# FFN channel units as three 256-column products in one PSUM bank, and another place for the input in SBUF

## The chip, the core and the metric

The kernel runs on one core of a Trainium2 chip. A core has five engines that run their own instruction streams and meet only at semaphores: TensorE (PE) multiplies matrices, ScalarE (ACT) applies functions, VectorE (DVE) does elementwise arithmetic, GpSimd (POOL) and SyncE (SP) do the rest; here SP starts all the DMA transfers. A matmul on PE has a stationary operand (the weights of the array, loaded by an instruction of its own, LDWEIGHTS, shown as PEld in the profile) and a moving operand that streams through the array, one column at a time. Both are read from SBUF, the on-chip memory of 128 partitions; the sum goes to PSUM, which has eight banks of 2 KB per partition (512 fp32 numbers each).

The metric is the device time of one execution in microseconds (us); lower is better.

## The reference

The reference is a decoder trunk of two layers over 256 tokens of width 1024. Each layer is a half-step SwiGLU feed-forward (FFN), a token mixer, and a second half-step FFN; a final norm ends it.

```
def swiglu(x, w_in, w_out):
    gate, up = jnp.split(x @ w_in, 2, axis=-1)
    return (jax.nn.silu(gate) * up) @ w_out
...
    for l in range(DEPTH):
        h = h + 0.5 * swiglu(rms_norm(h, ffn1_norm[l]), ffn1_w_in[l], ffn1_w_out[l])
        u = rms_norm(h, mix_norm[l])
        ...
        h = h + merged @ w_out[l]
        h = h + 0.5 * swiglu(rms_norm(h, ffn2_norm[l]), ffn2_w_in[l], ffn2_w_out[l])
    return rms_norm(h, final_norm)
```

The hidden width of the FFN is 2816. The mixer projects its normed input to many channels, runs a Mamba-2 branch and a gated DeltaNet branch on them, and merges the two. All is float32.

## The kernel before

**Precision.** PE takes float32 in a fast format (float32r) that keeps fewer bits. So each operand is split into a high and a low part, and a product `w * u` is computed as three: `wh * uh`, `wh * ul`, `wl * uh`. `mm3` (L287 to L289) does it with the activations as the stationary operand, `mm3w` (L292 to L294) with the weights as the stationary operand.

**The input.** Each of the four FFNs and two mixers begins with `norm_in`. It norms the 256 tokens, transposes them and writes their high and low parts to one tile, `uT`, of shape 128 partitions x 8 (blocks of 128 input channels, `KT`) x 2 (high, low) x 256 tokens. In a partition, the high and the low part of one block lie next to each other, so they can also be read as one run of 512 columns. `uT` is in the pool `cpool`, which is allocated ahead of the pools of the weights (`wpool`) and of the activations (`slots`, `s2`).

**The weights.** SP loads them in tiles of 128 x 1024 (`wraw`); ACT copies each one to `whi` and DVE subtracts to get `wlo`, both float32r, in five buffers each. `take()` hands out the next pair and has later ones loaded and split (up to five ahead). Weights come in the order of the products, so PE's program order is the order of everything.

**Products of the input.** There are two kinds. A token chunk (`tok_chunk`) has `uT` stationary, 128 tokens at a time, and 512 columns of weights moving: outputs `t0`, `t1` in the mixer, `f0`, `f1` at the start of an FFN. A channel chunk has 128 x 128 weights stationary and `uT` moving, so the output lies with channels in partitions. In the mixer that is `chan_chunk`: for each of two groups of 128 channels and each of the eight blocks, `mm3w`, which is three matmuls of 256 columns, into one half of a single PSUM bank (outputs `kk`, `qq`, `vv`, `zd`, `bc`, `xs`). In the FFN it is `chan_pair`: for each group and block one matmul of 512 columns (L342, `wh` with high and low part side by side) and one of 256 columns (L346, `wl` with the high part, onto the first 256 columns of the same bank), so each group of 128 channels fills a whole bank, and `both` adds the two halves afterwards.

**A channel unit of the FFN.** For each of the 20 units of an FFN, the first group of 128 channels is the gate and the second the up part. ACT copies the second half of the gate's bank to `sg`, DVE adds the first half, ACT applies SiLU; ACT copies the second half of the up bank to `g2`, DVE adds the first half, and DVE multiplies the two. Two units make one `g2`, which `split` turns into a high part `gh` and a low part `gl`, and `block_sums` into sums for a blocked product (`bsa`, `bsb`, `bsc`, `bsd`). The string `FFN` sets the order: `f` the token chunk, `c` a channel unit, `A` and `B` blocked products with w_out, `d` direct ones. An `A` uses channel units that ended at least two units before. The PSUM pool `accp` has four banks, taken in turn; the pool `trp` has the other four.

**The mixer.** The string `ORDER` is its order, written out by hand; the channel units there are followed by a convolution on ACT and DVE (tile `ca`).

The lines that the change touches:

Of the kernel before, what the change touches and what calls it, by code (L numbers as in the profile page):

```python
# [8 lines left out]
F32R = mybir.dt.float32r  # L9
# [7 lines left out]
P = 128  # L17
# [12 lines left out]
NRAW = 5  # L30
NSPL = 5
START = 2

# [18 lines left out]
def trunk_kernel(ctx, tc, x, wst, wsm, norms, lpar, rpar, cst, out):  # L52
# [12 lines left out]
    def act(o, i, func=AF.Copy, **kw):  # L65
        return A.activation(out=o, in_=i, func=func, **kw)  # L66

    def tt(o, a, b, op):
        return V.tensor_tensor(out=o, in0=a, in1=b, op=op)  # L69
# [18 lines left out]
    def accb(name):  # L88
        return accp.tile([P, 512], F32, tag="acc", name=name)
# [91 lines left out]
    def take():  # L181
        j = state["taken"]
        state["taken"] = j + 1
        ahead("loaded", min(plan[min(j + NSPL, n_forms) - 1][2] + NRAW - 1, n_raw), load)
        ahead("prepped", min(j + 1 if state["hold"] else j + NSPL, n_forms), prep)
        return halves.pop(j)
# [40 lines left out]
    Y = [cpool.tile([P, 512], F32, name=f"Y{i}") for i in range(2)]  # L227
    for y in Y:
        G.memset(y[:], 0.0)
    uT = cpool.tile([P, KT, 2, S], F32R, name="uT")  # L230
    uTh, uTl = uT[:, :, 0], uT[:, :, 1]

    def rstd_of(t):

# [25 lines left out]

    def norm_in(nw, add=None):

        for t in range(2):
            with tc.high_priority(offset=PRI), ExitStack() as behind:
                if add:
                    add(t)
                    if t == 0:
                        behind.enter_context(tc.issue_after(state["sums"][5].ins))
                ins, done = rms_chain(t, nw)
            if t == 0:  # L270
                state["hold"] = False
                n = state["taken"]
                if not add:
                    ahead("prepped", n + 1, prep)
                    with tc.issue_after(done[0].ins), tc.issue_after(done[1].ins):
                        ahead("prepped", n + START, prep)
                with tc.issue_after(ins.ins):
                    ahead("prepped", n + 2, prep)
                if add:
                    state["behind"][n + 2] = [d.ins for d in done]  # L280
            elif add:

                state["behind"][n + 4] = (state["square"].ins, ins.ins)
                state["input"] = done
# [28 lines left out]
    def chan_chunk(ps):  # L313

        ws = [take(), take()]
        for a in range(2):
            for q in range(2):
                wh, wl = ws[q]
                for k in range(4):
                    kt = 4 * q + k  # L320
                    c0 = k * 256 + a * P
                    mm3w(
                        ps[:, a * 256 : (a + 1) * 256],
                        wh[:, c0 : c0 + P],
                        wl[:, c0 : c0 + P],
                        uTh[:, kt, :],
                        uTl[:, kt, :],
                        kt == 0,
                        kt == KT - 1,
                    )  # L330

    def chan_pair(ps):


        ws = [take(), take()]
        for a in range(2):
            for q in range(2):
                wh, wl = ws[q]
                for k in range(4):
                    kt = 4 * q + k  # L340
                    c0 = k * 256 + a * P
                    PE.matmul(  # L342
                        ps[a][:], wh[:, c0 : c0 + P], uT[:, kt].rearrange("p o t -> p (o t)"),
                        start=kt == 0, stop=False,
                    )
                    PE.matmul(ps[a][:, 0:S], wl[:, c0 : c0 + P], uTh[:, kt, :], start=False, stop=kt == KT - 1)  # L346
            yield a

    def both(o, ps):
        act(o, ps[:, S : 2 * S])  # L350
        return tt(o, ps[:, 0:S], o, ALU.add)

    def out_chunks(ps, stat, ks, last, group=1, split=False, first=None):

# [86 lines left out]
    def ffn(nxt):  # L441
        gh = [slots.tile([P, 8, S], F32R, tag=t_, name="gh") for t_ in ("sA", "sB", "sC")]
        gl = [slots.tile([P, 8, S], F32R, tag=t_, name="gl") for t_ in ("sD", "sE", "sF")]

        bsa = slots.tile([P, 2, 2, 3, P], F32R, tag="sG", name="bsa")
        bsb = slots.tile([P, 16, P], F32R, tag="sH", name="bsb")
        bsc = slots.tile([P, 4, 2, P], F32R, tag="sI", name="bsc")
        bsd = s2.tile([P, 2, 2, P], F32R, tag="s2", name="bsd")
        bsb3 = bsb[:, 0:12].rearrange("p (i o j) t -> p i o j t", i=2, o=2)
        bsb1 = bsb[:, 12:16].rearrange("p (i o) t -> p i o t", i=2)  # L450

        def sums(p, j):

            q, i = (p - 1) // 2, (p - 1) % 2
            if j < 3:
                b = (bsa[:], bsb3)[q % 2]
                return b[:, i, 0, j, :], b[:, i, 1, j, :]
            b = (bsc[:, 0:2], bsc[:, 2:4], bsb1, bsd[:])[q]
            return b[:, i, 0, :], b[:, i, 1, :]

        def block_sums(p, g2):

            sf = tmp2("sf")
            a11, a21, a12, a22 = (g2[:, j * P : (j + 1) * P] for j in range(4))
# [12 lines left out]
            tt(l1, s4, f(h1), ALU.subtract)  # L477

        def split(k0, bv):
            oh = gh[k0 // 8][:, k0 % 8 : k0 % 8 + 2, :]  # L480
            ol = gl[k0 // 8][:, k0 % 8 : k0 % 8 + 2, :]
            act(oh, bv)
            tt(ol, bv, f(oh), ALU.subtract)

        def stat(k, t):
            return (gh[k // 8][:, k % 8, t * P : (t + 1) * P], gl[k // 8][:, k % 8, t * P : (t + 1) * P])

        ps = [accb("f0"), accb("f1")]
        tok_chunk(ps, range(KT))
        gt = []  # L490
        for t in range(2):
            sg = tmp2("sg")
            act(sg[:, 0:256], ps[t][:, 0:256], AF.Silu)
            tt(sg[:, 256:512], sg[:, 0:256], ps[t][:, 256:512], ALU.mult)
            gt.append(sg[:, 256:512])
        todo, pb, n = FFN[1:], {}, 0
        for c in range(FC - 1):
            g2 = tmp2("g2")
            for a in range(2):
                pc = [accb("fc"), accb("fc")]  # L500
                sg = s2.tile([P, S], F32, tag="ca", name="sg", bufs=2)
                gv = g2[:, a * S : (a + 1) * S]
                for i in chan_pair(pc):
                    if i == 0:
                        both(sg[:], pc[0])
                        act(sg[:], sg[:], AF.Silu)
                both(gv, pc[1])
                tt(gv, sg[:], gv, ALU.mult)
                todo = todo[1:]
                if c == 0 and a == 0:  # L510
                    bank = trb("gT")
                    for k in range(2):
                        for t in range(2):
                            PE.transpose(bank[:, k * S + t * P : k * S + (t + 1) * P], gt[t][:, k * P : (k + 1) * P], ident)
                    split(0, bank[:].rearrange("p (k t) -> p k t", k=2))
            split(2 * c + 2, g2[:].rearrange("p (k t) -> p k t", k=2))
            if c + 1 <= PAIRS[-1][-1]:
                block_sums(c + 1, g2)
            if todo[0] == "A":
                if not pb:  # L520
                    pb.update({i: trb(f"p{i}") for i in (1, 6, 5, 7)})
                four = [
                    (pb[1], lambda p: stat(2 * p, 0), PAIRS[n]),
                    (pb[5], lambda p: sums(p, 0), PAIRS[n]),
                    (pb[7], lambda p: sums(p, 2), PAIRS[n]),
                    (pb[6], lambda p: sums(p, 1), PAIRS[n]),
                ]
                block_products(four, n == 0, n == len(PAIRS) - 1)
                todo = todo[1:]
                n += 1  # L530
        po = [[accb("o"), accb("o")] for _ in range(2)]

        return close_blocks(po, stat, sums, pb, nxt)
# [841 lines left out]
```

## Time and profile before

| | |
|---|---|
| median of 3 runs | 1570.2 us (1566.86 to 1570.4) |
| span of the profiled execution, first to last instruction | 1565.8 us |
| what lies around the span, against the median | 4.4 us |
| mean granted TensorE clock | 0.999 |
| PE busy | 1545.0 us, 10152 matmuls |
| DVE busy | 1302.4 us |
| ACT busy | 999.8 us |
| DMA | 292.99 MB, 55.2% of the DMA engines' time |

The profiled execution's time is its span, 1565.8 us, and the little that lies ahead of the first and behind the last instruction; the three runs are 1.1 to 4.6 us above the span.

How to read it: "busy" of PE is counted from the start of each matmul to its modelled end, and matmuls overlap, so a matmul of 512 columns shown with 390 ns does not take 390 ns of PE's time. What a stream of matmuls takes is the distance from one start to the next, and that is read from the start times in the timeline. In a row of the groups, "L342 PE MATMUL fc<-uT,whi 128\*128 128x512 f32 x1280" is line 342, output `fc`, operands `uT` and `whi`, a stationary operand of 128 x 128, 512 moving columns, 1280 instructions; then busy time, mean ns of one, and the idle time of the engine ahead of them. The four FFNs begin with their token chunks at about 10, 604, 787 and 1379 us; the mixers begin at about 193 and 969 us.

### The profile page before, as it was taken

To read this page: it belongs to the slowest core of one execution; us is meant where nothing else is said; L and a number is where in the kernel's file an instruction comes from. 1 tells how busy PE (TensorE), PEld (TensorE's weight loads), DVE (VectorE), ACT (ScalarE), POOL (GpSimd) and SP (SyncE) were. 2 spreads that over 40 slices of the span, in tenths; PEclk is the share of its full clock that TensorE was granted. 3 is DMA by queue.
4 is the path that set the end of the run, shared out by engine and by line. 5 is a ranking of instruction groups with operands and counts; after the bars stand their busy time and mean duration, and the time that the engine had idled before them with its cause. 6 is when DMAs were issued, how large, how long until landed. Compare 5 with 4: busy or idle time off the path is not lost.

```text
span 1565.8 us, 26672 instructions
## 1 busy us (share of the span) xinstructions
PE 1545.0 (99%) x10152; PEld 1342.0 (86%) x10152; DVE 1302.4 (83%) x2048; ACT 999.8 (64%) x1694; POOL 53.2 (3%) x60
## 2 busy tenths in 40 slices
PE   8999999999999999999999999999999999999998
PEld 6888779999888888888788887899998888888886
DVE  6889969957899766899878998699579996679897
ACT  6666668766675655666566676686656666466664
POOL 0000010000000000000000001010000000000000
PEclk9999999999999999999999999999999999999999
DMA  8565565553455555465765566555336546555553
GB/s 298 197 214 188 195 212 173 178 158 118 174 207 173 177 205 196 159 210 177 262 204 187 168 198 223 189 189 189 116 123 213 177 166 212 201 175 166 198 189 134
DMA packets 94215, 292.99 MB, mean 187 GB/s; under 512 B 22325, under 2 KB 23301, under 8 KB 93062
## 3 DMA queue, kind: packets, MB, share of 16 engines
q1 hardware_dynamic: 94086, 291.29, 55.2%
q8 instruction: 79, 1.29, 0.3%
q14 instruction: 50, 0.41, 0.1%
HBM read 289.33 MB, written 1.92 MB: 186 GB/s over the span
## 4 chain that ended last, share of the span: by engine, by line
PE 76%; DVE 13%; DMA 5%; issue 3%; ACT 2%; POOL 1%; SPq 0%; POOLq 0%; DVEq 0%; ACTq 0%
PE fc L342 15%; PE fc L346 8%; DVE wlo L69 7%; PE t L287 3%; PE t L288 3%; PE t L289 3%; DMA wraw<-in_wst_dram 3%; PE b L289 3%; PE b L288 3%; PE b L287 2%; PE xs L292 2%; PE xs L293 2%; PE xs L294 2%; PE o L288 1%; PE o L289 1%
## 5 line engine op out<-in xcount | busy, mean ns | idle before, releaser
L69 DVE TENSOR_TENSOR wlo<-wraw,whi 128x1024 fp32r<-128x1024 f32 x488 | 591.0, 1221 | 139.8 <-ACT whi L66 136.1
L66 ACT ACTIVATE whi<-wraw 128x1024 fp32r<-128x1024 f32 x488 | 511.6, 1057 | 176.4 <-PE b L289 29.8
L342 PE MATMUL fc<-uT,whi 128*128 128x512 f32 x1280 | 445.5, 391 | 0.0
L346 PE MATMUL fc<-uT,wlo 128*128 128x256 f32 x1280 | 360.9, 282 | 0.0
L342 PEld LDWEIGHTS fc<-uT,whi 128*128 128x128 f32 x1280 | 240.3, 188 | 50.7
L346 PEld LDWEIGHTS fc<-uT,wlo 128*128 128x128 f32 x1280 | 241.8, 189 | 0.8
L287 PE MATMUL t<-whi,uT 128*128 128x512 f32 x256 | 102.9, 403 | 0.0
L288 PE MATMUL t<-wlo,uT 128*128 128x512 f32 x256 | 101.5, 396 | 0.2 <-DVE wlo L69 0.2
L289 PE MATMUL t<-whi,uT 128*128 128x512 f32 x256 | 101.5, 397 | 0.0
L66 ACT ACTIVATE whi<-wfirst 128x1024 fp32r<-128x1024 f32 x64 | 67.8, 1059 | 29.7 <-DVE wfirst L69 20.4
L66 ACT ACTIVATE sg<-fc 128x256 f32<-128x256 f32 x80 | 30.6, 382 | 82.3 <-PE fc L346 82.3
L69 DVE TENSOR_TENSOR wlo<-wfirst,whi 128x1024 fp32r<-128x1024 f32 x64 | 78.1, 1220 | 2.0 <-ACT whi L66 1.9
L287 PE MATMUL b<-whi,bh 128*128 128x512 f32 x192 | 76.1, 398 | 0.0
L288 PE MATMUL b<-wlo,bh 128*128 128x512 f32 x192 | 74.9, 390 | 0.0
L289 PE MATMUL b<-whi,bl 128*128 128x512 f32 x192 | 74.3, 394 | 0.3 <-DVE bl L69 0.3
L292 PE MATMUL xs<-uT,whi 128*128 128x256 f32 x256 | 73.1, 286 | 0.0
L294 PE MATMUL xs<-uT,wlo 128*128 128x256 f32 x256 | 71.6, 280 | 0.0
L293 PE MATMUL xs<-uT,whi 128*128 128x256 f32 x256 | 71.4, 279 | 0.0
L288 PE MATMUL o<-wlo,gh 128*128 128x512 f32 x160 | 64.6, 404 | 2.6 <-DVE wlo L69 2.5
L69 DVE TENSOR_TENSOR wfirst<-wraw,wfirst 128x1024 f32<-128x1024 f32 x48 | 58.6, 1220 | 8.9 <-DMA wraw<-in_wst_dram 8.9
L289 PE MATMUL o<-whi,gl 128*128 128x512 f32 x160 | 62.5, 391 | 0.0
L287 PE MATMUL o<-whi,gh 128*128 128x512 f32 x160 | 62.1, 392 | 0.0
(317 smaller groups left out, 3424.5 us busy)
## 6 DMA issues: line engine op xcount, KB each, us to landing
wraw<-in_wst_dram SPq DMA_DIRECT2D x504, 512.0 KB, 4.5
wfirst<-in_wst_dram SPq DMA_DIRECT2D x16, 512.0 KB, 5.8
dc<-rdram SPq DMA_DIRECT2D x8, 1024.0 KB, 8.4
nw<-in_norms_dram SPq DMA_DIRECT2D x6, 512.0 KB, 6.2
gb<-rdram SPq DMA_DIRECT2D x8, 256.0 KB, 5.3
h<-in_x_dram SPq DMA_DIRECT2D x4, 256.0 KB, 5.7
out_dram<-fo SPq DMA_DIRECT2D x4, 256.0 KB, 2.1
dq<-X SPq DMA_DIRECT2D x2, 256.0 KB, 5.0
```

The costliest lines, as they stand in the source:

```text
L66: return A.activation(out=o, in_=i, func=func, **kw)
L69: return V.tensor_tensor(out=o, in0=a, in1=b, op=op)
L287: PE.matmul(ps, lh, rh, start=start, stop=False)
L288: PE.matmul(ps, lh, rl, start=False, stop=False)
L289: return PE.matmul(ps, ll, rh, start=False, stop=stop)
L292: PE.matmul(ps, wh, mh, start=start, stop=False)
L293: PE.matmul(ps, wh, ml, start=False, stop=False)
L294: PE.matmul(ps, wl, mh, start=False, stop=stop)
L342: PE.matmul(ps[a][:], wh[:, c0 : c0 + P], uT[:, kt].rearrange("p o t -> p (o t)"), start=kt == 0, stop=False,)
L346: PE.matmul(ps[a][:, 0:S], wl[:, c0 : c0 + P], uTh[:, kt, :], start=False, stop=kt == KT - 1)
```

## The change

1. The FFN's channel units use `chan_chunk`, as the mixer's do: three matmuls of 256 columns in place of one of 512 and one of 256, with gate and up in the two halves of one bank. `chan_pair` and `both` go. SiLU reads the gate from PSUM, and the multiplication reads the up part from PSUM.
2. The tile of the input has 64 more elements per partition (256 bytes), and the input lies 40 elements (160 bytes) behind its start, in each of the six norms. With this the weight tiles lie 64 bytes behind the input modulo 256. All tiles allocated after it move by 256 bytes, so their places modulo 256, and the distances between them, stay.

```
+PLACES = 6 * [40]
...
-    uT = cpool.tile([P, KT, 2, S], F32R, name="uT")
-    uTh, uTl = uT[:, :, 0], uT[:, :, 1]
+    uW = cpool.tile([P, KT * 2 * S + 64], F32R, name="uW")
+    uT = uTh = uTl = None
+    places = list(PLACES)
+
+    def place_input():
+        nonlocal uT, uTh, uTl
+        o = places.pop(0)
+        uT = uW[:, o : o + KT * 2 * S].rearrange("p (k o t) -> p k o t", k=KT, o=2)
+        uTh, uTl = uT[:, :, 0], uT[:, :, 1]
...
     def norm_in(nw, add=None):
 
+        place_input()
...
-    def chan_pair(ps):
...
-                    PE.matmul(
-                        ps[a][:], wh[:, c0 : c0 + P], uT[:, kt].rearrange("p o t -> p (o t)"),
-                        start=kt == 0, stop=False,
-                    )
-                    PE.matmul(ps[a][:, 0:S], wl[:, c0 : c0 + P], uTh[:, kt, :], start=False, stop=kt == KT - 1)
...
-    def both(o, ps):
-        act(o, ps[:, S : 2 * S])
-        return tt(o, ps[:, 0:S], o, ALU.add)
...
-                pc = [accb("fc"), accb("fc")]
+                ps = accb("fc")
+                chan_chunk(ps)
                 sg = s2.tile([P, S], F32, tag="ca", name="sg", bufs=2)
-                gv = g2[:, a * S : (a + 1) * S]
-                for i in chan_pair(pc):
-                    if i == 0:
-                        both(sg[:], pc[0])
-                        act(sg[:], sg[:], AF.Silu)
-                both(gv, pc[1])
-                tt(gv, sg[:], gv, ALU.mult)
+                act(sg[:], ps[:, 0:S], AF.Silu)
+                tt(g2[:, a * S : (a + 1) * S], sg[:], ps[:, S : 2 * S], ALU.mult)
```

`chan_chunk`, which stays as it is:

```
        ws = [take(), take()]
        for a in range(2):
            for q in range(2):
                wh, wl = ws[q]
                for k in range(4):
                    kt = 4 * q + k
                    c0 = k * 256 + a * P
                    mm3w(
                        ps[:, a * 256 : (a + 1) * 256],
                        wh[:, c0 : c0 + P], wl[:, c0 : c0 + P],
                        uTh[:, kt, :], uTl[:, kt, :],
                        kt == 0, kt == KT - 1,
                    )
```

More of the change, by code (lines that the diff above doesn't have):

```diff
@@ L330, in chan_chunk @@
                     )
-    def chan_pair(ps):
[L335 to L342, printed above, removed]
-                        ps[a][:], wh[:, c0 : c0 + P], uT[:, kt].rearrange("p o t -> p (o t)"),
-                        start=kt == 0, stop=False,
-                    )
-                    PE.matmul(ps[a][:, 0:S], wl[:, c0 : c0 + P], uTh[:, kt, :], start=False, stop=kt == KT - 1)
-            yield a
-    def both(o, ps):
-        act(o, ps[:, S : 2 * S])
-        return tt(o, ps[:, 0:S], o, ALU.add)
     def out_chunks(ps, stat, ks, last, group=1, split=False, first=None):
```

## The prediction

> **What bounds the kernel now.** I read the page's busy times and its chain first.
>
> ```profile
> span 1565.8 us, 26672 instructions
> PE 1545.0 (99%) x10152; PEld 1342.0 (86%) x10152; DVE 1302.4 (83%) x2048; ACT 999.8 (64%) x1694; POOL 53.2 (3%) x60
> PEclk9999999999999999999999999999999999999999
> PE 76%; DVE 13%; DMA 5%; issue 3%; ACT 2%; POOL 1%; SPq 0%; POOLq 0%; DVEq 0%; ACTq 0%
> ```
>
> PE is busy almost throughout, the clock is full everywhere, and three quarters of the chain that ends last are PE's. So the question is how fast PE's stream of matmuls goes, and whether the next engine, DVE at 83%, lets it go faster. The stretches, by the windows (span of time; then busy us and count of PE, PEld, DVE, ACT, POOL; clock; DMA):
>
> ```profile
> 33.00:69.00 36.00, 36.00 (x209) 31.91 (x209) 30.39 (x56) 22.39 (x41) 0.00 (x0) 1.00 0.61 206
> 234.00:262.00 28.00, 28.00 (x242) 28.00 (x242) 26.10 (x55) 21.99 (x37) 0.00 (x0) 1.00 0.57 194
> 440.00:505.00 65.00, 64.94 (x502) 57.14 (x500) 62.46 (x81) 42.35 (x56) 3.07 (x2) 1.00 0.55 187
> ```
>
> The first is FFN channel units alone: PE never pauses, DVE has 30.39 of 36 us. The second is mixer channel units: DVE 26.10 of 28. The third is the densest part of the mixer for DVE, 62.46 of 65: there DVE sets the pace as much as PE does.
>
> The groups say how many matmuls read the input, which the change moves:
>
> ```profile
> L342 PE MATMUL fc<-uT,whi 128*128 128x512 f32 x1280 | 445.5, 391 | 0.0
> L346 PE MATMUL fc<-uT,wlo 128*128 128x256 f32 x1280 | 360.9, 282 | 0.0
> L292 PE MATMUL xs<-uT,whi 128*128 128x256 f32 x256 | 73.1, 286 | 0.0
> L292 PE MATMUL bc<-uT,whi 128*128 128x256 f32 x128 | 36.7, 287 | 0.0
> L292 PE MATMUL zd<-uT,whi 128*128 128x256 f32 x128 | 36.3, 284 | 0.0
> L292 PE MATMUL vv<-uT,whi 128*128 128x256 f32 x128 | 36.0, 281 | 0.0
> L292 PE MATMUL qq<-uT,whi 128*128 128x256 f32 x128 | 36.0, 281 | 0.0
> L292 PE MATMUL kk<-uT,whi 128*128 128x256 f32 x128 | 35.9, 281 | 0.0
> L287 PE MATMUL t<-whi,uT 128*128 128x512 f32 x256 | 102.9, 403 | 0.0
> L287 PE MATMUL f<-whi,uT 128*128 128x512 f32 x64 | 26.4, 415 | 0.5 <-ACT uT L66 0.5
> ```
>
> FFN channel units: 1280 pairs of 512 and 256 columns. Mixer channel units: the six L292 rows are 896 matmuls, and L293 and L294 have as many, so 2688 of 256 columns. Token chunks: 256 + 64 on each of three lines, 960 of 512 columns with `uT` stationary.
>
> **What each kind costs now.** From start times in the timeline (start us, modelled us), first row of a stretch and first row behind it:
>
> ```profile
> 130.01 0.40 PE L342 MATMUL fc<-uT,whi 128*128 128x512 f32 x1
> 141.12 0.39 PE L287 MATMUL p<-whi,gh 128*128 128x512 f32 x1
> 319.76 0.28 PE L292 MATMUL zd<-uT,whi 128*128 128x256 f32 x1
> 325.36 0.28 PE L292 MATMUL bc<-uT,whi 128*128 128x256 f32 x1
> 439.06 0.40 PE L287 MATMUL t<-whi,uT 128*128 128x512 f32 x1
> 450.27 0.38 PE L1045 MATMUL xsb<-cs,xsT 128*128 128x128 f32 x2
> 98.27 0.39 PE L287 MATMUL p<-whi,bsb 128*128 128x512 f32 x1
> 102.35 0.40 PE L342 MATMUL fc<-uT,whi 128*128 128x512 f32 x1
> ```
>
> - FFN: two units, 32 pairs, in 141.12 - 130.01 = 11.11 us: 347.2 ns for a pair (768 columns).
> - Mixer: one unit, 48 matmuls of 256, in 5.60 us: 116.7 ns each, 350.0 for the same 768 columns.
> - Token chunks: two units, 48 matmuls of 512, in 11.21 us: 233.5 ns each.
> - Blocked products: 18 matmuls of 512, in 4.08 us: 226.7 ns each.
>
> The last two are the same matmul in shape, type and clock, and differ by 6.8 ns. What differs is where the operands lie. After the change the weights are 64 bytes behind the input modulo 256, and the input moves by 160, so before they are 64 + 160 = 224 bytes behind it, or 32 ahead: 32 off a multiple of 64. `bsb` and the weights are a whole multiple of 256 bytes apart, as the tiles between them have 4096, 6144 and 8192 bytes. So in this trace a half-step distance costs time and a whole one costs none, which also fits the other rows: take 226.7 / 512 = 0.4428 ns a column as the price of columns alone, and 768 columns cost 340.0. The FFN pair is 7.2 over that with two matmuls, the mixer's three are 10.0 over: 3.6 and 3.3 ns for a matmul with `uT` moving, 6.8 with `uT` stationary.
>
> **The change, part by part.**
>
> *Three products for a pair, alone:* the same columns, one more matmul and one more weight load (1280 in all). At the mixer's price, 350.0 - 347.2 = 2.8 ns more a pair: 1280 x 2.8 = +3.6 us, on the path, as PE has no pause there.
>
> *The new place:* 64 bytes is a whole step of 64, so if the step is what counts, each kind falls to the price of columns: 340.0 for three, 113.3 for 256, 226.7 for 512. No row shows this distance: the aligned rows are all at 0 modulo 256. Bounds from the nearest rows: 0 for a matmul as in the `p` rows, and 6.8 for each as in the `t` rows, the dearest that a distance costs here. A price below 0 has no row behind it, though nothing excludes it. I take 0, since at 64, as at 0, both operands cross 64-byte steps together. Then:
>
> - FFN: 1280 x (347.2 - 340.0) = 9.2 us, the 3.6 of the first part already in it.
> - Mixer channel units: 2688 x (116.7 - 113.3) = 9.1 us.
> - Token chunks: 960 x (233.5 - 226.7) = 6.5 us.
>
> Together 24.8 us of PE time. Two deductions. In 440:505 DVE has no room, and its counterpart in the second mixer neither; 64 matmuls on each of the three channel lines and about 43 of `t` lie in it: 192 x 3.4 + 43 x 6.8 = 0.95 us, twice, 1.9. And an aligned stream takes a few matmuls to settle:
>
> ```profile
> 96.89 0.39 PE L287 MATMUL p<-whi,gh 128*128 128x512 f32 x1
> 97.12 0.40 PE L288 MATMUL p<-wlo,gh 128*128 128x512 f32 x1
> 97.36 0.39 PE L289 MATMUL p<-whi,gl 128*128 128x512 f32 x1
> 97.59 0.39 PE L287 MATMUL p<-whi,gh 128*128 128x512 f32 x1
> ```
>
> The first three take 0.70 us, 0.02 over three at the settled price (0.68). The mixers have 2688 / 48 = 56 channel and 768 / 24 = 32 token units; if each begins unsettled, that is 88 x 0.02 = 1.8 us. Net: 24.8 - 1.9 - 1.8 = 21.1.
>
> *The evacuation:* ACT and DVE lose work in the 80 units.
>
> ```profile
> L66 ACT ACTIVATE sg<-sg 128x256 f32<-128x256 f32 x80 | 33.0, 413 | 22.4 <-DVE sg L69 21.9
> L66 ACT ACTIVATE sg<-fc 128x256 f32<-128x256 f32 x80 | 30.6, 382 | 82.3 <-PE fc L346 82.3
> L66 ACT ACTIVATE g<-fc 128x256 f32<-128x256 f32 x80 | 29.4, 367 | 0.1
> L69 DVE TENSOR_TENSOR g<-sg,g 128x256 f32<-128x256 f32 x80 | 33.7, 421 | 0.5
> L69 DVE TENSOR_TENSOR sg<-fc,sg 128x256 f32<-128x256 f32 x80 | 33.6, 420 | 4.1 <-ACT sg L66 4.0
> L69 DVE TENSOR_TENSOR g<-fc,g 128x256 f32<-128x256 f32 x80 | 33.5, 419 | 0.0
> L66 ACT ACTIVATE sg<-f 128x256 f32<-128x256 f32 x8 | 3.1, 384 | 3.6 <-PE f L289 3.6
> ```
>
> ACT has one SiLU from PSUM (384, as `sg<-f`) in place of 382 + 413 + 367: 62 us less over the kernel. DVE has one multiplication of about 420 in place of three: 67 us less. I cost both at 0: PE has no pause in 33:69, so there is nothing for it to gain; the worth is that DVE, at 30.39 of 36, doesn't become the bound when PE runs 2% faster.
>
> *One bank for gate and up:* ACT may now have to wait for all 48 matmuls, where it had its first bank after half of them; the 82.3 us of idle time ahead of `sg<-fc` would grow, and the splits of weights queued behind it on ACT would come later. Cost 0: splits run up to five tiles ahead, two and a half units, and an `A` reads units that ended two units before. Without that cover it is 384 + 420 = 0.8 us a unit. Four banks now hold four units, where they held two, so a bank comes free earlier than before.
>
> *The rest:* `place_input` issues nothing. No DMA changes; PE's faster pace asks for the same bytes in 1.4% less time, with the DMA engines at 0.61. Tiles behind the input move by 256 bytes, so their distances stay.
>
> The sum against the profiled execution: span 1565.8 - 21.1 = 1544.7, and with the 4.4 us by which the median of the three runs is over that span 1549.1. I predict 1549.
>
> **The rivals.**
>
> *The place does nothing.* The difference between `t` and `p` rows would then come from the token chunks' own pattern of operands, and only the third product counts: +3.6 us, 1574. Against it stands that mixer and FFN channel units, with the operands' parts exchanged, are over the price of columns too. Chance 0.14. The Trainium skill speaks for it, in "SBUF — State Buffer", "A bandwidth-pool intuition that's wrong (but worth ruling out)": PE's weight loads have a read port of their own, independent of the moving operand's, so by that page the distance between the two shouldn't matter. In "TensorE: Matmul & The Clock Gate", "Back-to-back issue gap", a warm matmul alone takes its columns at 2.4 GHz and 2.5 ns; by that page the estimate is 2.5 ns for each of the 1280 added, +3.2 us, and nothing for the place. The trace doesn't agree with either: the same shape takes 226.7 or 233.5, both over that page's 215.8.
>
> *64 is a bad distance (slower).* Both operands would meet at the same step of a store with more than one step to its cycle, on every matmul. For it speaks that an aligned stream that hasn't settled pays too (0.24 us for one of 512, from 97.12 to 97.36). At the dearest row's price, 6.8, a 256-column matmul takes 120.1: FFN 1280 x (360.3 - 347.2) = +16.8, mixer 2688 x 3.4 = +9.1, token chunks 0; 1596. It decides as soon as a matmul of 256 costs over 347.2 / 3 = 115.7 in the FFN. Against it: `p` settles within three matmuls. Chance 0.14.
>
> *Half of it.* Streams of 256 settle only partly, at 115: FFN 1280 x (347.2 - 345.0) = 2.8, mixer 2688 x 1.7 = 4.6, token chunks 6.5 less half for DVE: -11; 1559. Chance 0.12.
>
> **How the numbers follow.** The forecast has 0.60, and its own range is 1541 (the full 24.8, and 4 of the 67 us that DVE loses, since 13% of the chain is DVE's) to 1558 (DVE holds back most of the mixer's share: 9.2 for the FFN's units, 1.3 for `f` and 2 more are left). A change under 0.3% (4.7 us) can't be told from none here. Faster: forecast and half, 0.72. "Does nothing" at 1574 is mostly inside 0.3%, a third over it: same 0.10, slower 0.04 + 0.14 = 0.18. The range 1541 to 1577 leaves out the bad distance (0.14) and a little below, under 2 in 10.
>
> **What would show it.** FFN channel units at 113.3 ns from start to start (5.44 us a unit, now 5.55), mixer units at 5.44 (now 5.60), `t` at 226.7; 11432 matmuls; ACT about 62 and DVE about 67 us less busy; no waits of PE for `sg` or `g`. Wrong if a 256-column start comes every 116 ns or more; or if PE is fast and shows new pauses in the mixer, at DVE's `wlo` or `ca`.

## The result, and the profile after

The change makes the kernel slower by a little: 1574.2 us (median of 6 runs, 1572.8 to 1577.6) against 1567.4 (6 runs, 1565.0 to 1570.4) on the same chip. The ratio is 1.0043, with a 95% interval of 1.0031 to 1.0056: 6.8 us. The forecast was 21 us faster.

The page of the changed kernel, its span, busy times, granted clock and chain:

```profile
span 1573.0 us, 28904 instructions
PE 1544.0 (98%) x11432; PEld 1393.4 (89%) x11432; DVE 1254.2 (80%) x1888; ACT 950.7 (60%) x1534; POOL 53.8 (3%) x60
PEclk9999999999999999999999999999999999999999
PE 68%; DVE 14%; DMA 7%; issue 5%; ACT 4%; POOL 1%; SPq 0%; POOLq 0%; ACTq 0%; DVEq 0%
```

The count of matmuls is as forecast and the clock is full as before. PE's share of the chain fell from 76 to 68%, and DMA, issue and ACT gained: PE waits more often. The evacuation, by which ACT and DVE take a unit's sums out of PSUM, is now these groups (busy us, mean ns, idle before):

```profile
L70 DVE TENSOR_TENSOR g<-sg,fc 128x256 f32<-128x256 f32 x80 | 33.2, 415 | 0.0
L67 ACT ACTIVATE sg<-fc 128x256 f32<-128x256 f32 x80 | 29.2, 365 | 0.0
```

Against the six rows of before, ACT's three have become 29.2 us (63.8 less) and DVE's three 33.2 (67.6 less). On the page the two engines' busy times fall by 49 and 48 us only, since neighbouring records overlap; added up one by one, the records fall by 61 and 65.

Where PE's time went, in the timeline of the changed kernel (start us, modelled us). A stretch is a run of matmuls of one kind with no other work of PE in it; its pace is the time from one start to the next. Each pair of rows is the first of a stretch and the first behind it: FFN units behind `p` (192 matmuls), behind `gT` in the first and the third FFN (336 each), two mixer units (96), two token units (48):

```profile
104.14 0.28 PE L301 MATMUL fc<-uW,whi 128*128 128x256 f32 x1
...
126.75 0.39 PE L296 MATMUL p<-whi,gh 128*128 128x512 f32 x1
...
30.95 0.36 PE L301 MATMUL fc<-uW,whi 128*128 128x256 f32 x1
...
70.60 0.39 PE L296 MATMUL p<-whi,gh 128*128 128x512 f32 x1
...
810.09 0.37 PE L301 MATMUL fc<-uW,whi 128*128 128x256 f32 x1
...
848.27 0.39 PE L296 MATMUL p<-whi,gh 128*128 128x512 f32 x1
...
253.40 0.28 PE L301 MATMUL kk<-uW,whi 128*128 128x256 f32 x1
...
264.28 0.38 PE L704 MATMUL turned<-cs,kP 128*128 128x128 f32 x2
...
440.31 0.39 PE L296 MATMUL t<-whi,uW 128*128 128x512 f32 x1
...
451.30 0.38 PE L1029 MATMUL xsb<-cs,xsT 128*128 128x128 f32 x2
```

- Behind `p`: 22.61 us for 192, 117.8 ns each; 353.3 for three, where the pair cost 347.2. All 16 stretches behind `p` are so.
- Behind `gT`: 39.65 us in the first FFN (118.0 ns), 38.18 in the third (113.6, and 113.3 once it has settled). The second and fourth are as the first. The same instructions at the same distance have two paces.
- `kk`: 10.88 us for 96, 113.3 ns, as forecast (116.7 before). `t`: 10.99 us for 48, 229.0 ns, two thirds of the way from 233.5 to 226.7.

Summed over the trace from start to start, `fc` went from 444.5 to 450.6 us, `kk` and `qq` together from 90.2 to 87.5, `t` from 186.8 to 184.1; `vv`, `zd`, `bc` and `xs` stayed at 233, with units at 113.3 and units at 117.8 ns among them. And `o`, the products that close an FFN or a mixer, which nothing in the diff touches, went from 184.2 to 189.9. These make +5.9 of the 7.2 us between the spans; the rest is in small parts. The waits of before (waiter <- releaser: us in total, times, longest us), by the view of waits:

```profile
ACT sg L66 <- PE fc L346: 82.3, 64, 1.7
ACT whi L66 <- PE fc L342: 26.4, 46, 0.9
PEld o L288 <- DVE wlo L69: 10.5, 21, 1.1
DVE wfirst L69 <- DMA wraw<-in_wst_dram: 8.9, 11, 1.6
```

and of after:

```profile
ACT whi L67 <- PE fc L302: 146.9, 121, 3.1
DVE wfirst L70 <- DMA wraw<-in_wst_dram: 18.7, 10, 3.6
PEld o L297 <- DVE wlo L70: 16.1, 23, 1.4
```

ACT waited for PE's `fc` before too, 82.3 us ahead of `sg<-fc` and 26.4 ahead of weight splits; now all of it, 146.9 us, is ahead of weight splits. A kernel below, with DVE's order edited, still has 136.8 us of them and an `o` as short as before, so they aren't what `o` loses. The other two rows are: `o` waits longer for `wlo`, and DVE waits longer for weights from DRAM. DVE at the last closing (the end of an FFN, with its `o`), before:

```profile
1519.30 1.23 DVE L69 TENSOR_TENSOR wlo<-wraw,whi 128x1024 fp32r<-128x1024 f32 x1 [0.37 <-ACT whi L66]
1520.44 0.42 DVE L69 TENSOR_TENSOR g<-fc,g 128x256 f32<-128x256 f32 x1
1522.43 1.23 DVE L69 TENSOR_TENSOR wfirst<-wraw,wfirst 128x1024 f32<-128x1024 f32 x1 [1.57 <-DMA wraw<-in_wst_dram]
```

and after:

```profile
1524.93 1.23 DVE L70 TENSOR_TENSOR wfirst<-wraw,wfirst 128x1024 f32<-128x1024 f32 x1 [3.60 <-DMA wraw<-in_wst_dram]
1526.08 1.22 DVE L70 TENSOR_TENSOR wlo<-wraw,whi 128x1024 fp32r<-128x1024 f32 x1
```

The subtraction `wfirst<-wraw,wfirst` prepares the second of the four blocked products `B`. In the order that was laid out for DVE before, the split of the first block's last weight stands ahead of it; in the changed kernel the order came out the other way round, in all four closings, and here DVE sits 3.60 us at the subtraction with the split behind it. Whether the fewer evacuation instructions or the added product turned the order isn't shown, as no run has one without the other.

### The profile page after: what moved, and what is told of

It reads as the page before. It is cut to its first block, busy times and chain, and to the rows that moved or that the text cites. A ratio compares the mean times of both kernels' runs of the same rounds, so it can differ in the third digit from the quotient of the medians.

```text
span 1573.0 us, 28904 instructions
## 1 busy us (share of the span) xinstructions
PE 1544.0 (98%) x11432; PEld 1393.4 (89%) x11432; DVE 1254.2 (80%) x1888; ACT 950.7 (60%) x1534; POOL 53.8 (3%) x60
## 3 DMA queue, kind: packets, MB, share of 16 engines
q8 instruction: 89, 1.46, 0.4%
## 4 chain that ended last, share of the span: by engine, by line
PE 68%; DVE 14%; DMA 7%; issue 5%; ACT 4%; POOL 1%; SPq 0%; POOLq 0%; ACTq 0%; DVEq 0%
PE fc L301 9%; PE fc L302 9%; PE fc L303 9%; DVE wlo L70 7%; DMA wraw<-in_wst_dram 4%; PE b L298 3%; PE t L297 3%; PE t L296 2%; PE t L298 2%; PE b L297 2%; PE b L296 2%; DVE ca L73 2%; ACT whi L67 2%; PE p L297 2%; PE p L298 2%
## 5 line engine op out<-in xcount | busy, mean ns | idle before, releaser
L301 PE MATMUL fc<-uW,whi 128*128 128x256 f32 x1280 | 359.2, 281 | 0.0
L303 PE MATMUL fc<-uW,wlo 128*128 128x256 f32 x1280 | 358.9, 280 | 0.0
L302 PE MATMUL fc<-uW,whi 128*128 128x256 f32 x1280 | 358.9, 280 | 0.0
L303 PEld LDWEIGHTS fc<-uW,wlo 128*128 128x128 f32 x1280 | 243.6, 190 | 0.0
L301 PEld LDWEIGHTS fc<-uW,whi 128*128 128x128 f32 x1280 | 241.7, 189 | 0.8
L302 PEld LDWEIGHTS fc<-uW,whi 128*128 128x128 f32 x1280 | 240.3, 188 | 0.8
L296 PE MATMUL t<-whi,uW 128*128 128x512 f32 x256 | 102.1, 400 | 0.0
L297 PE MATMUL t<-wlo,uW 128*128 128x512 f32 x256 | 100.6, 393 | 0.4 <-DVE wlo L70 0.4
L298 PE MATMUL t<-whi,uW 128*128 128x512 f32 x256 | 100.7, 393 | 0.0
L70 DVE TENSOR_TENSOR wfirst<-wraw,wfirst 128x1024 f32<-128x1024 f32 x48 | 58.7, 1222 | 19.1 <-DMA wraw<-in_wst_dram 18.7
L301 PE MATMUL xs<-uW,whi 128*128 128x256 f32 x256 | 72.7, 284 | 0.0
L303 PE MATMUL xs<-uW,wlo 128*128 128x256 f32 x256 | 71.1, 278 | 0.0
L302 PE MATMUL xs<-uW,whi 128*128 128x256 f32 x256 | 71.0, 277 | 0.0
```

The lines of the kernel that those rows point to most:

```text
L296: PE.matmul(ps, lh, rh, start=start, stop=False)
L297: PE.matmul(ps, lh, rl, start=False, stop=False)
L298: return PE.matmul(ps, ll, rh, start=False, stop=stop)
L301: PE.matmul(ps, wh, mh, start=start, stop=False)
L302: PE.matmul(ps, wh, ml, start=False, stop=False)
L303: PE.matmul(ps, wl, mh, start=False, stop=stop)
```

## The experiments

Ratios are against the kernel before on the same chip, with 95% intervals; a time given without a ratio is that of a single execution. "Standstill" is PE's time at `o` above its pace, in the four closings: 7.7 us before, 13.3 after.

**The place alone.** Pairs as before, the input at the new place (distance 64).

```
+PLACES = 6 * [40]
...
-    uT = cpool.tile([P, KT, 2, S], F32R, name="uT")
+    uW = cpool.tile([P, KT * 2 * S + 64], F32R, name="uW")
...
+        place_input()
```

> The input at its new place (weights 64 bytes behind it modulo 256), with the FFN's pairs of 512 and 256 columns and their evacuation as before. Theory A, that a stream of 256-column matmuls has two settled paces at this distance (113.3 and 117.8 ns) and that the FFN fell into the slow one, while the place itself is good: a pair takes 340 to 344 ns (347 before), token chunks 229, and the waits of the closing products (output o, 9.3 us before, 15.1 after) stay near 9; about 8 us faster than before. Rival B, that the place is bad for FFN channel units: a pair takes 350 or more and the kernel is no faster than before. If the longer waits at o come from the place, they are 15 us here too.

1571.5 us, ratio 1.0007 (0.9995 to 1.0019). A stretch of 64 pairs:

```profile
103.85 0.39 PE L351 MATMUL fc<-uW,whi 128*128 128x512 f32 x1
...
126.46 0.39 PE L296 MATMUL p<-whi,gh 128*128 128x512 f32 x1
```

22.61 us, 353.3 ns for a pair, 6.1 over before. `fc` sums to 452.5 us (+8.0), `kk`, `qq` and `t` to 4.0 less together, standstills are 8.4. The forecast's idea that 64 bytes are a whole step falls for pairs as they ran here, all of them at this pace; whether a pair has a faster pace at 64 as well, as it has at 0 (last experiment), one trace doesn't show. The place does change every stage, for the worse with pairs and for the better in the mixer, and the total hides it. The Trainium skill, "SBUF — State Buffer", "A bandwidth-pool intuition that's wrong (but worth ruling out)", gives weight loads a read port of their own, by which the place would do nothing: the total agrees (1.0007), its parts don't (+8.0 and -4.0 us).

**Three products alone.** The changed kernel with the input where it was (distance 224).

```
-PLACES = 6 * [40]
+PLACES = 6 * [0]
```

> Three products of 256 columns and the new evacuation, with the input at its old distance (weights 224 bytes behind it modulo 256). Theory A: the FFN's stream goes as the mixer's did before, 116.7 ns a matmul in rotation (350 for three, 347 for the pair), so 3.6 us of PE time more than before; if the longer waits at o (15.1 us after, 9.3 before) come from the new evacuation, they are here too, and the kernel is 9 us slower than before, slower than with the new place. Rival B: the place cost the time, and this kernel is faster than the changed one.

1582.0 us, ratio 1.0079 (1.0062 to 1.0096). A stretch of 192:

```profile
103.67 0.28 PE L301 MATMUL fc<-uW,whi 128*128 128x256 f32 x1
...
126.08 0.39 PE L296 MATMUL p<-whi,gh 128*128 128x512 f32 x1
```

22.41 us, 116.7 ns each, in every stretch. `fc` is 448.4 us, +3.9. It is slower than the changed kernel, so with three products the place does help, but not in the FFN: `fc` is 2 us lower here, and what the changed kernel gains is in `kk` and `qq` (2.7), `t` (4.1) and `o` (2.5). And `o` is 192.4, +8.2: the closings are worse here too, so they don't come from the place.

**Other distances.** Three products with the input at another place in each FFN and mixer, in two kernels.

```
-PLACES = 6 * [40]
+PLACES = [56, 56, 8, 24, 8, 48]
...
+PLACES = [16, 24, 32, 36, 48, 44]
```

> Three products, with another distance in each stage: weights behind the input modulo 256 by 0 in the first FFN and the first mixer, 192 in the second FFN, 128 in the third FFN, 192 in the second mixer, 32 in the last FFN. Theory A': multiples of 64 give either of two settled paces, 113.3 or 117 to 118 ns, by the start of each stretch, and 32 gives 116.7 in rotation. Rival: 0, 128 or 192 always settle at 113.3 and only 64 has the slow state.

> Three products, with other distances: 160 in the first FFN, 128 in the first mixer, 96 in the second FFN, 80 in the third FFN, 32 in the second mixer, 48 in the last FFN. If half steps of 64 bytes are what costs: 160, 96 and 32 run at 116.7 ns in rotation, 128 at 113.3 or 118; quarter steps (80, 48) lie between, by the same. Rival: the distance doesn't matter in steps of 64 at all, and all show the same 113 to 118.

1593.3 and 1593.6 us. FFN units in the first, at distance 0, and token units at 0:

```profile
105.60 0.28 PE L301 MATMUL fc<-uW,whi 128*128 128x256 f32 x1
...
128.63 0.40 PE L296 MATMUL p<-whi,gh 128*128 128x512 f32 x1
...
446.86 0.40 PE L296 MATMUL t<-whi,uW 128*128 128x512 f32 x1
...
457.77 0.49 PE L1029 MATMUL xsb<-cs,xsT 128*128 128x128 f32 x3
```

23.03 / 192 = 119.9 ns, and 10.91 / 48 = 227.3 (226.7 settled). So at 0 the same place is the best for 512 columns with the input stationary and the worst for 256 with the input moving. A 256-column product in the FFNs took 120.0 at 0 and 160, 120.0 behind `p` and 118.7 behind `gT` at 128, 119.2 at 48 and 80, 118.7 at 96, 118.3 at 32, 117.8 at 192, 116.7 at 224, and 113.3 or 117.8 at 64. Multiples of 64 (0, 64, 128, 192) are not alike. But for 64 and 224, each distance was seen in one FFN of one execution. And every run moved the input and left the weights, so "distance" is a name here: the input's own place modulo 256 would sort the figures as well.

**The last split of the gate's products later.** On ACT, `gh` waits for DVE's `g` with weight splits behind it (36.2 us for all such waits); here it is issued one block later.

```
...
-            split(2 * c + 2, g2[:].rearrange("p (k t) -> p k t", k=2))
+            if c < FC - 2:
+                split(2 * c + 2, g2[:].rearrange("p (k t) -> p k t", k=2))
...
+            if n == 1:
+                with tc.issue_after(state["hi"].ins):
+                    late()
...
```

> The changed kernel, with the last split of the gate's products (gh, gl) in each FFN issued one block later, so that on ACT both of the first block's weight splits stand ahead of gh, as they do in the kernel before. The time that PE stands still for o in the four closings is 13.4 us in the changed kernel and 7.8 us in the kernel before. Theory A, the changed kernel's closings lose time because ACT sits at gh, waiting for DVE's g, with weight splits queued behind it: the standstills for o fall to about 8 us and the time to about 1569 us. Theory B, they lose it because DVE sits at two joins (u) that wait for the DMA of raw weights, ahead of its own weight splits: the joins stay where they are, the standstills stay at 12 to 14 us and the time at 1574 us or over.

1573.6 us, ratio 1.0021 (1.0011 to 1.0031); standstills 13.3 us, `o` 190.0. In the trace `gh` now stands behind the split that it stood ahead of, and `o` is no shorter. So Theory A falls: `gh`'s place in ACT's order is not the cause. The time is lower than the changed kernel's all the same; in this trace all four stretches behind `gT` are at 113.3 ns, which the edit doesn't touch.

**Two banks.** Gate and up in a bank each.

```
-                ps = accb("fc")
-                chan_chunk(ps)
+                ps2 = [accb("fc"), accb("fc")]
+                chan_chunk(None, ps2)
...
```

> The changed kernel, with gate and up in two PSUM banks of 256 columns each, as the kernel before had two banks for a unit. Theory A, the pace of the channel units is set by where weights and input lie, not by the bank: the start-to-start time stays at 113.3 or 117.8 ns and the time within 0.3% of 1574 us. Theory B, eight matmuls that add into one half of a bank while ACT and DVE are to read the other half, or the waits on a whole unit's bank, cost the pace: the units go at 113.3 ns (5.44 us) throughout and the time falls by up to 7 us, 80 units by 0.2 us less half of it, as DVE's closings remain.

1574.1 us, ratio 1.0017 (1.0005 to 1.0029). Stretches behind `p` at 117.8 ns, standstills 14.0 us: the single bank costs nothing that the trace shows. The stretches behind `gT` are fast in all four FFNs here too, which makes `fc` 4.0 us less than in the changed kernel's trace and can explain the lower time.

**The changed kernel once more**, without an edit:

> The changed kernel once more, for a second profile. If a stretch's pace is set by the program alone, the stretches of 336 matmuls behind gT come out as in the first profile: 117.8 ns in the first, second and fourth FFN, 113.3 in the third. If it is set by the phase in which an execution happens to start the stretch, those behind gT change and those behind p, which follow PE's own products without a pause, stay at 117.8 ns.

1570.5 us. Behind `gT` in the first FFN:

```profile
30.50 0.36 PE L301 MATMUL fc<-uW,whi 128*128 128x256 f32 x1
...
68.69 0.39 PE L296 MATMUL p<-whi,gh 128*128 128x512 f32 x1
```

38.19 us in place of 39.65, and so in all four FFNs; the 16 behind `p` stay at 117.8 ns. The span is 1568.7, 4.3 us under the first profile's, which is three times the 1.46. So the pace behind `gT` belongs to the execution (or to the chip it ran on, which was not held fixed), not to the program, and four such stretches are worth up to 5.8 us; that behind `p` repeats. Part of the 6.8 us of the result can be this; how much isn't known, as one of its six runs has a trace.

**A small product ahead of a stretch.** 8, 20, 64 and 72 columns in the first to the fourth FFN.

```
...
+        if nudge:
+            PE.matmul(ps[:, 0:nudge], ws[0][0][:, 0:P], uTh[:, 0, 0:nudge], start=True, stop=True)
...
```

> The changed kernel, with one small product more (128 partitions by 8, 20, 64 and 72 columns in the first to the fourth FFN) ahead of each stretch of channel units that follows other work of PE; its result is written over by the unit's first product. Theory A, at distance 64 the stream of 256 columns has two settled states, 113.3 and 117.8 ns, and what precedes a stretch (the phase of its start) decides which: with one of the four widths or more an FFN is fast throughout (units of 5.44 us), and others stay slow (5.65 us); an FFN that is fast throughout is 20 units x 0.21 = 4 us shorter. Theory B, the pace follows from something that goes on beside it (DMA writes, DVE and ACT reads): the four FFNs stay as they are, about 5.65 us a unit, whatever the width.

1572.3 us. Behind `p`, with 8 columns (first FFN) and with 72 (fourth):

```profile
103.68 0.17 PE L328 MATMUL fc<-uW,whi 128*128 128x8 f32 x1
103.71 0.36 PE L303 MATMUL fc<-uW,whi 128*128 128x256 f32 x1
...
126.41 0.40 PE L298 MATMUL p<-whi,gh 128*128 128x512 f32 x1
...
1472.91 0.20 PE L328 MATMUL fc<-uW,whi 128*128 128x72 f32 x1
1472.94 0.36 PE L303 MATMUL fc<-uW,whi 128*128 128x256 f32 x1
...
1494.79 0.39 PE L298 MATMUL p<-whi,gh 128*128 128x512 f32 x1
```

192 matmuls in 22.70 us behind 8 columns and 21.85 behind 72. All four stretches behind `p` are slow with 8 and with 20 columns, all four fast with 64 and with 72, each width in one FFN of this one execution. With the same units, weights and place, what runs ahead decides the pace, so it isn't set by the DMA, DVE or ACT beside it. That the phase of the start is what counts is the reading that fits; the runs don't show the phase itself.

**72 columns in all four FFNs.** `NUDGES = 4 * [72]`.

> The changed kernel, with a product of 72 columns more ahead of each stretch of channel units that follows f, gT or p, in all four FFNs; its result is written over by the unit's first product. Theory A, the phase of a stretch's start decides its settled pace, and 72 columns put it in the fast one behind p: the stretches of 192 and 96 matmuls go at 113.3 ns in all four FFNs, fc sums to about 438 us in place of 450.6, and the time is 10 to 12 us under the changed kernel's, about 1563 us, faster than the kernel before. Theory B, PE's gain is taken by weight splits and DMA that don't keep up: the pace is 113.3 ns, but standstills for o or for whi grow, and the time stays above 1568 us.

1568.6 us, ratio 1.0000 (0.9987 to 1.0013). All 16 stretches behind `p` go at 113.3 ns; three of four behind `gT` are slow in this trace. `fc` is 443.2 us, 7.4 less than in the changed kernel and not the 12 of Theory A, and standstills are 14.6 us. The trace is of the slowest of the ten runs, 1574.3 us, and its three slow stretches behind `gT` cost 4.4; without them `fc` would be 438.8, about what Theory A named. By the median, the fast pace behind `p` alone brings the kernel back to the time before.

**The subtraction behind the split.** The edit in the order of DVE alone, at the new place and then at the old one.

```
             elif kind == "q4":
-                less(0, 3, 0)
+                state["q4"] = state.get("q4", -1) + 1
+                if state["q4"] % 4 == 1:
+                    with tc.issue_after(state["q5"].ins):
+                        less(0, 3, 0)
+                else:
+                    less(0, 3, 0)
-            tt(lo[:], r[:], f(hi[:]), ALU.subtract)
+            low = tt(lo[:], r[:], f(hi[:]), ALU.subtract)
+            if kind == "q5":
+                state["q5"] = low
```

> The changed kernel, with one subtraction of DVE in each closing (wfirst<-wraw,wfirst of the second block, which waits for the DMA of a raw weight) issued behind the weight split that it stood ahead of, as in the kernel before. Theory A, that wait at the head of DVE's queue holds up the split, the split's raw buffer comes free late, and the loads and splits behind it are late for o: PE's standstills for o in the four closings fall from 13.4 us to about 8 us, and the time from 1574 to about 1569 us. Theory B, the closings are late because DVE and ACT come to them late whatever the order: standstills and time stay within 1 us of the changed kernel.

> Three products at the old place (distance 224), with the subtraction of the second block issued behind the split. Without that move it lost 12.5 us to the kernel before: fc +3.9, o +8.2. If the order on DVE makes the closings' part, o falls by 6 to 8 us and the time is about 1575 us, 5 us over the kernel before; if the third product itself brings the closings late, the time stays above 1579 us.

At the new place: 1566.2 us, ratio 0.9983 (0.9971 to 0.9995). At the old place: 1572.8 us, 1.0018 (1.0009 to 1.0028), where it was 1.0079. DVE at the last closing, and the waits, at the new place:

```profile
1514.87 1.23 DVE L70 TENSOR_TENSOR wlo<-wraw,whi 128x1024 fp32r<-128x1024 f32 x1 [1.72 <-ACT whi L67]
1516.97 1.23 DVE L70 TENSOR_TENSOR wfirst<-wraw,wfirst 128x1024 f32<-128x1024 f32 x1 [0.88 <-DMA wraw<-in_wst_dram]
...
ACT whi L67 <- PE fc L309: 136.8, 118, 3.1
PEld o L304 <- DVE wlo L70: 7.5, 11, 1.1
DVE wfirst L70 <- DMA wraw<-in_wst_dram: 5.5, 7, 1.6
```

DVE's waits for weights fall from 18.7 to 5.5 us, `o`'s for `wlo` from 16.1 to 7.5, standstills from 13.3 to 7.2, and `o` from 189.9 to 183.5. At the old place `o` falls from 192.4 to 183.4, 9.0 us, and the span from 1580.9 to 1571.8. So the order that came out with this one edit is worth 6.4 us of `o` at the new place and 9.0 at the old one. The total at the new place fell by more, but in this trace all four stretches behind `gT` are fast, which makes `fc` 4.2 us less and has nothing to do with the edit. With the subtraction `gh` and a join of the blocks (`u`, on DVE) moved back some places as well; `gh` alone did nothing, the join was not tried by itself, so the subtraction's share apart from the join's isn't shown.

**Both edits**, and both with the extra product only behind `p`:

```
-        nudge, kick = nudges.pop(0), True
+        nudge, kick = nudges.pop(0), False
...
-                kick = c == 0 and a == 0
+                kick = False
```

> The two edits together: the extra product of 72 columns ahead of each stretch of channel units in the FFNs, and the subtraction of the second block behind the split. If the two losses are separate, they add: 10 to 12 us for the pace and about 5 us for the closings, about 1558 us. If a faster PE brings the closings' loads too late anyway, the second edit brings under 2 us on top of the first, about 1562 us.

> The two edits together, with the extra product of 72 columns only ahead of the stretches that follow p, 16 in place of 24. If the stretches behind f and gT find their own phase, their pace changes from FFN to FFN as in the changed kernel, and the time is within 2 us of the kernel with the two edits, about 1560 us, 0.6% under the kernel before; stretches behind p stay at 113.3 ns.

1559.7 us, ratio 0.9946 (0.9930 to 0.9963), and 1561.1 us, ratio 0.9937 (0.9924 to 0.9951). The two losses are separate and add, and three products at the new place then beat the kernel before by 0.5 to 0.6%. `fc` is 440.6 and 439.8 us. The stretches behind `f` and `gT` still differ from FFN to FFN, with the product ahead of them and without.

**Extra products in the mixers too**, ahead of `vv`, `zd`, `bc` and `xs`:

```
-            chan_chunk(ps)
+            chan_chunk(ps, 72)
```

> The two edits together, and the extra product of 72 columns also ahead of the mixers' units vv, zd, bc and xs, which go at 117.8 ns at least in part in the changed kernel. If DVE leaves room there, vv, zd and xs fall to 113.3 ns and the time is up to 6 us under that of the two edits alone; if DVE sets the pace in the mixers, the gain is under 2 us.

1573.1 us, ratio 1.0019 (1.0006 to 1.0031): over 11 us worse than the two edits alone, which no theory had. `vv`, `zd`, `bc` and `xs` take 5.8 us more instead of less, and `oT` and `yT`, which follow them, 6.3. About 4 of the 5.8 are the 40 extra products themselves: the first unit of `vv` settles at 113.3 ns in both kernels and takes 5.66 us with one and 5.56 without, 0.10 more. Nor do 72 columns put every unit into the fast pace here (`zd` behind `vv` went from 113.3 to 117.8 ns), and the work behind them comes later; which order or wait makes `oT` and `yT` late stays open.

**The place in the mixers alone.** FFNs with pairs at 224, as before the change.

```
-PLACES = 6 * [40]
+PLACES = [0, 40, 0, 0, 40, 0]
```

(against the first experiment's kernel)

> The kernel before, FFNs with pairs and the input where it was (distance 224), and the input moved to distance 64 in the two mixers alone. By the traces so far the mixers are the part that gains: channel units of kk and qq at 113.3 in place of 116.7 ns and t at 229 in place of 233.5, 2.3 us for a mixer between its first and last marks. Theory A, the place's worth depends on which operand moves and on the columns, so mixers keep their gain and FFNs lose nothing: 4 to 6 us faster than the kernel before, about 1565 us. Theory B, the mixer's gain is given back at its end, where DVE sets the pace: within 0.3% of the kernel before.

1565.3 us, ratio 0.9971 (0.9959 to 0.9983): 4.5 us faster. `kk` and `qq` take 2.7 us less, `t` 1.7, `vv`, `zd`, `bc` and `xs` 1.7, and `o` 1.7 more; `fc` is unchanged at 444.5.

**Pairs at other distances.** `PLACES = [56, 24, 8, 48, 56, 24]` in the same kernel.

> The kernel before, pairs in the FFNs, with the input at other distances: 0, 192, 32 and 128 in the first to the fourth FFN, 128 and 0 in the mixers. Theory A, the price belongs to the distance and the shape, so a pair costs a 512-column product and a 256-column one, each at its own price: with 120.0, 117.8, 118.3 and 120.0 ns for the 256 (as three products took them) and 226.7 to 235 for the 512, all between 345 and 355 ns. Theory B, the old place was a chance among equals: all four FFNs within 1 ns of 346.8.

1576.3 us. Behind `p`, pairs take 353.1 ns at 0, 349.0 at 192, 346.8 at 32 and 350.8 at 128; behind `gT` 347.5, 353.9, 354.1 and 351.8, so pairs have more than one pace too. At 0, behind `gT` (112 pairs) and behind `p` (64 pairs):

```profile
29.72 0.48 PE L351 MATMUL fc<-uW,whi 128*128 128x512 f32 x1
...
68.64 0.39 PE L296 MATMUL p<-whi,gh 128*128 128x512 f32 x1
...
102.19 0.39 PE L351 MATMUL fc<-uW,whi 128*128 128x512 f32 x1
...
124.78 0.40 PE L296 MATMUL p<-whi,gh 128*128 128x512 f32 x1
```

38.92 / 112 = 347.5 ns (346.7 once settled), and 22.59 / 64 = 353.0. No place beats the old one by more than 0.4 ns. The price belongs to distance and shape, as Theory A has it, and to the pace that a stretch falls into: the sum of the two products' own at 0, 226.7 + 120.0 = 346.7, is met behind `gT` and missed by 6 behind `p`.

## Why the prediction was wrong

**What bounds the kernel** was right for the units: there the time follows PE's stream. So was every count. In the closings PE stands still, 7.7 us before and 13.3 after, mostly for `wlo`.

**Three products alone, +3.6 us:** right. `fc` rose by 3.9 at the old place, and the units went at the mixer's 116.7 ns to the digit. The Trainium skill's issue gap ("TensorE: Matmul & The Clock Gate", "Back-to-back issue gap") gave an estimate of +3.2; the trace agrees within 0.7.

**The new place, "64 bytes is a whole step of 64, so if the step is what counts, each kind falls to the price of columns":** this step failed, in two inferences.
- From one kind to another. The price without loss was read from 512-column products at distance 0. It does hold for token chunks at 0 (226.7). But a 256-column product with the input moving costs 120.0 there, as much as at any distance tried. That "both operands cross 64-byte steps together" is no advantage for it.
- From one pace to all. At 64 the 113.3 ns exist, and the forecast size is right where a stream finds them (`kk`, `qq`, a stretch behind `gT`). But a second pace, 117.8, is as stable, and the FFN stretches behind `p` are in it, all 80 in the five traces of three products at 64 without an extra product. The prediction knew unsettled starts and priced them at 0.02 us a unit, as if every stream settled into the same pace.

FFN: forecast -9.2 with the third product's cost in it, measured +6.1. Mixer channel units: -9.1, measured -2.7 for `kk` and `qq` and -0.5 for the others. Token chunks: -6.5, measured -2.7, as 229.0 is not 226.7.

**The evacuation, 62 and 67 us off ACT and DVE, cost 0:** the sizes were right (63.8 and 67.6), the cost was not. "PE has no pause in 33:69, so there is nothing for it to gain" looked for a gain in the units. The loss came in the closings, where the order of DVE's queue was laid out anew, and a subtraction that waits for DMA moved ahead of a split: +5.7 us in `o`. With the edit in that order `o` is 183.5 us, less than before the change; what turned it, fewer evacuation instructions or one more product, stays open. The prediction never asked what that order would be.

**One bank, cost 0:** right as far as the traces show: two banks changed neither the pace behind `p` nor the closings, and ACT's longer wait was not what they lost.

**The rivals.** "The place does nothing" named 1574 us, and the time is there, but by another way: the place costs or gains in every stage. "64 is a bad distance" had the right sign and the right point of decision (115.7 ns for a 256-column product; it took 117.8), and too high a price (120.1). "Half of it", streams that settle only partly, is nearest in mechanism; but it put their pace at 115, on the cheap side of 115.7. The sign to look for, a 256-column start every 116 ns or more, is what the profile showed. That 1574.2 lies inside the wide range, 1541 to 1577, is luck: it comes of a gain in the mixers, a loss in the FFN's units and a loss in the closings, and the prediction had no loss in the closings at all.

## What to carry to other kernels

A price read from one kind of matmul at one placement holds for that kind at that placement; before it is summed over thousands of instructions, time the very shape at the very distance, and look whether its pace is the same in all stretches. When a change adds or removes instructions on engines with a planned order, compare the new order around every wait for DMA: an instruction that waits at the head of a queue holds up what stands behind it. And a total that doesn't move can be two effects that cancel, so sum each stage apart.

## What was not expected of the hardware

- A stream of 256-column float32r products at distance 64 has two settled paces, 113.3 and 117.8 ns. Which one a stretch takes differs from FFN to FFN and from execution to execution behind `gT`, and can be chosen behind `p` by one small product: 8 or 20 columns leave it at 117.8, 64 or 72 bring 113.3 (all 64 stretches behind `p` of the four kernels that had 72 columns throughout). What sets the pace stays open; the phase of the start is a reading that fits. Pairs have two settled paces as well, 346.7 and 353.3 ns at distance 0.
- The distance of weights and input modulo 256 bytes, changed by moving the input alone, moves a 256-column product between 113.3 and 120.0 ns, and a 512-column one with the input stationary between 226.7 (at 0), 229.0 (at 64) and 233.5 (at 224): 0 is the dearest place for the one and the cheapest for the other.
